# A decoder trunk's attention in another order of steps: the next head's logits first, the splits of k and q alternating between two banks, copies to high parts on GpSimd

## The chip, the cores and the metric

The kernel runs on one core of a Trainium2 chip, in one launch. The metric is the device time of that core in microseconds (us), start to end of the program. A core has TensorE (PE in the rows: matmuls and transposes, written to PSUM), VectorE (DVE), ScalarE (ACT), GpSimd (POOL) and SyncE (SP), which issues the DMAs. Each engine works through its own list of instructions in order and waits on semaphores for the others.

## The reference

Two layers of a decoder trunk on 512 tokens of width 1024, all in float32. Layer 0 mixes tokens with a gated MLP, layer 1 with attention, and each has a SwiGLU feed-forward network. What the change touches is the attention of layer 1:

```python
N_HEADS = 16; HEAD_DIM = 64; Q_BLOCK = 128; S = 512
q, k   = rms_norm(q, q_norm_g), rms_norm(k, k_norm_g)      # per head
gate   = sigmoid(h @ w_qg[:, D:])
logits = q @ k.T * HEAD_DIM**-0.5 + dcum[:, None] - dcum[None, :]
logits = where(key <= query, logits, -inf)
p      = softmax(logits)
o      = p @ v
y      = (o * gate) @ w_o
```

`dcum` is the running sum of log forget gates, one number for each head and token.

## The kernel before, in words

Every float32 matrix product is made of three matmuls in a rounded 32-bit format: each operand is split into a high part (a rounded copy) and a low part (what the rounding left), and high times high, high times low and low times high are summed in PSUM. So nearly every operand costs a copy and a subtraction on an engine besides TensorE.

The attention works on the 16 heads as eight pairs. `v`, `k` (tile `kn`) and `q` (tile `qn`) lie in SBUF with the tokens across the partitions; a pair takes 128 columns. These are the steps, with the names of their tokens in the table `ORDER` and the lines of the kernel before:

- `stack` (token `z0` for k, `z1` for q; L1066 to 1088): four transposes on TensorE (L1071) bring k or q of a pair into one PSUM bank, `ps_z`. Then, for each head of the pair, ScalarE copies the high part (L1085 for k, L1081 for q), VectorE subtracts for the low part (L1086, L1082), and GpSimd copies the high part to a second place (L1087). A small DMA puts the rows of `dcum` below it (L1078). k's bank comes from the two buffers `ps_t`, q's from the two buffers `ps_s`.
- `score` (`s0` to `s3`, one for each block of 128 queries, with 128 to 512 keys; L1090 to 1104): two matmuls into a `ps_s` bank (L1098, L1099); VectorE adds the mask, writes the negated logits `pr` and takes their minimum `mn` (L1102); ScalarE makes the exponentials and their sum (L1103).
- `trans` (`t0` to `t3`, one for each block of 128 keys; L1106 to 1122): transposes of the exponentials (L1113), into `acc` banks for t0 and t1 and `ps_t` banks for t2 and t3; ScalarE copies the high part `pt` (L1120), VectorE subtracts for the low part (L1121).
- `pv` (`v0` to `v3`): probabilities times v (L1133), summed in one `acc` bank for the head.
- `gather` (`g`): the head's result from PSUM to the columns of v that are no longer needed, by a ScalarE copy (L1141) and a VectorE addition (L1142).
- `R`, `T`, `B`: the reciprocals of the sums of both heads of a pair, as three small VectorE instructions (L1147, L1149, L1150), their transposes on TensorE (L1157), copied by ScalarE (L1159), and a matmul that spreads them (L1164), which VectorE multiplies into the gate (L1166).
- `L` and `f`: `gate_mm` loads and splits a pair's gate weights (the high part on VectorE, L118, the low part on GpSimd, L120); their 24 matmuls (L1048) are fillers, handed out one by one wherever an `f` stands. The 24th is followed by the gate's tanh on ScalarE (L1052).
- `V`: `prep_v` splits v of the next pair (L1061 on ScalarE, L1062 on GpSimd). `C`: the gate is multiplied in on GpSimd (L1176). `H`: the result is split for the output projection (L1183 on VectorE, L1184 on GpSimd).

`ORDER` has one line for the even head of a pair and one for the odd head. The loop issues the steps in that order, and `pin` keeps the marked instructions in that order on their engines; unmarked ones (the split of the gate weights) are placed by the scheduler. In the line of head i the score tokens are those of head i+1, and in the line of the even head `z` is the pair after. The loop begins after the projection of q (`moving` over `w_q`), whose head norm is the chain L143 to L154 on VectorE and L981 on GpSimd; the output projection (L1258 to 1260) follows it.

Of the kernel before, what the change touches and what calls it, by code (L numbers as in the profile page):

```python
# [18 lines left out]
P = 128  # L19
D = 1024  # L20
S = 512
# [29 lines left out]


ORDER = (
    "f f B f f f g t1 C f t0 f f V t2 t3 s0 f s1 f f f v0 v1 H s2 s3 v2 z0 v3 f f",
    "f z1 f R L t1 t3 g f f t0 f t2 f T s0 s1 f f f f v0 s2 s3 v1 v2 v3",
)

TRANS_BANK = "aapp"
# [7 lines left out]
def tile_yoco_trunk(ctx: ExitStack, tc: tile.TileContext, x, c, cols, ada_t, kv_ada_t,  # L66
# [799 lines left out]
    with tc.tile_pool(name="att", bufs=1) as tp:  # L866
# [171 lines left out]

        def gate_mm(p_):

            hi, lo = load_split(w_gate[p_], lo_eng=nc.gpsimd, hi_eng=nc.vector)
            box = []

            def step(kt, z):
                if not box:
                    box.append(acc.tile([P, 512], F32, name="acc"))
                cs = slice(kt * P, kt * P + P)
                pin(MM(box[0], (hi, hi, lo)[z][:, cs], h[z == 1][kt], start=kt + z == 0,  # L1048
                       stop=kt == KT - 1 and z == 2))
                if kt == KT - 1 and z == 2:  # L1050
                    ge = tp.tile([P, S], F32, name="ge", bufs=2)
                    pin(ACT(ge, box[0], AF.Tanh, scale=0.5))  # L1052
                    st["ge", p_] = ge
            fill.extend(lambda kt=kt, z=z: step(kt, z) for kt in range(KT) for z in range(3))

        def prep_v(p_):

            cs2 = slice(p_ * P, (p_ + 1) * P)
            vv = tp.tile([P, NT, 4, HD], F32R, name="vv", bufs=2)
            v4 = v[:, :, cs2].rearrange("p n (h d) -> p n h d", d=HD)  # L1060
            pin(ACT(vv[:, :, 0::3, :], v4, AF.Copy))  # L1061
            pin(nc.gpsimd.tensor_tensor(vv[:, :, 1:3, :], v4, f32(vv[:, :, 0::3, :]), sub))  # L1062
            st["vv", p_] = vv
            st["ls", p_] = tp.tile([P, NT, 2], F32, name="lsum", bufs=2)

        def stack(z, p_):  # L1066


            ps = aux.tile([P, NT, P], F32, name="ps_z", tag=("ps_t", "ps_s")[z])
            for n in range(NT):  # L1070
                pin(nc.tensor.transpose(ps[:, n, :], pair((kn, qn)[z], p_)[:, n, :], ident))  # L1071
            for e in range(2):
                i = 2 * p_ + e
                hs = slice(e * HD, (e + 1) * HD)
                src = flat(ps)[hs]
                t1 = tp.tile([P, S], F32R, name=f"st{z}1", bufs=2)
                t2 = tp.tile([HD + 4, S], F32R, name=f"st{z}2", bufs=2)
                nc.sync.dma_start(f32(t2[HD:]), f32(dT[z][4 * i:4 * i + 4]))  # L1078
                if z:
                    hi, dup, lo = (t1[HD:], t2[:HD], t1[:HD]) if e else (t2[:HD], t1[HD:], t1[:HD])  # L1080
                    pin(ACT(hi, src, AF.Copy))  # L1081
                    pin(TT(lo, src, f32(hi), sub))  # L1082
                else:
                    hi, dup, lo = t1[hs], t1[(1 - e) * HD:(2 - e) * HD], t2[:HD]
                    pin(ACT(hi, src, AF.Copy, scale=kqc[hs]))  # L1085
                    pin(STT(lo, src, kqc[hs], f32(hi), mul, sub))  # L1086
                pin(nc.gpsimd.tensor_copy(dup, f32(hi)))  # L1087
                st["kq"[z], i] = t1, t2

        def score(i, n):  # L1090

            p_, e = divmod(i, 2)
            (k1, k2), (q1, q2) = st["k", i], st["q", i]
            ns = slice(n * P, n * P + P)
            w = (n + 1) * P
            wm = max(w, 256)
            ps = aux.tile([P, 512], F32, name="ps_s")
            pin(MM(ps[:, :wm], q1[:, ns], k1[:, :wm], start=True, stop=False))  # L1098
            pin(MM(ps[:, :wm], q2[:, ns], k2[:, :wm], start=False, stop=True))  # L1099
            t = tp.tile([P, w], F32, name=f"pr{n}")  # L1100
            mn = small.tile([P, 1], F32, name="mn", bufs=4)
            pin(nc.vector.tensor_tensor_reduce(t, ps[:, :w], mask[:, S - w:], 1.0, BIG, add, ALU.min, mn))  # L1102
            pin(ACT(t, t, AF.Exp, bias=mn, scale=-1.0, accum_out=st["ls", p_][:, n, e:e + 1]))  # L1103
            st["pr", i, n] = t
# [73 lines left out]
        def close_hl(p_, eng=nc.gpsimd):  # L1178
            o = out_cols(p_)
            if p_ % 4 == 0:  # L1180
                for t in (oh, ol):
                    t.append(outer.tile([P, NT, 512], F32R, name="oh", tag="qk", bufs=4))
            pin(nc.vector.tensor_copy(pair(oh, p_), o))  # L1183
            pin(eng.tensor_tensor(pair(ol, p_), o, f32(pair(oh, p_)), sub))  # L1184

        moving([w_q[0, i] for i in range(4)], KT, 512, hl(h), lambda n, ps: eq(n, ps, 0), n_bg=0)
# [1 line left out]

        def first(i):
            if i == 2:  # L1190
                stack(0, 0)
                stack(1, 0)
            if i == 3:
                for n in range(NT):
                    score(0, n)
        moving([w_q[1, i] for i in range(4)], KT, 512, hl(h), lambda n, ps: eq(n, ps, 1), n_bg=0, extra=first)
        gate_mm(0)
        for i in range(NH):
            p_, e = divmod(i, 2)
            nx, more = i + 1 < NH, p_ + 1 < NH // 2  # L1200
            for tok in ORDER[e].split():
                z = int(tok[1:] or 0)
                tok = tok[0]
                if tok == "f":
                    filler(1)
                elif tok == "z" and more:
                    stack(z, p_ + 1)
                elif tok == "s" and nx:
                    score(i + 1, z)
                elif tok == "t":  # L1210
# [144 lines left out]
```

## Time and profile before

| | |
|---|---|
| time, median of 3 runs | 1394.09 us (1391.73 to 1397.08) |
| profiled execution | 1392.18 us, its span from the first to the last instruction 1390.5 us |
| TensorE busy | 1331.2 us, 96% of the span |
| VectorE, ScalarE, GpSimd busy | 886.3, 577.1, 244.3 us |
| mean granted TensorE clock | 0.988 of full speed |

In the page's forty slices TensorE is below nine tenths in slices 25 to 28 alone, apart from the first; that is the attention. "Busy" of TensorE includes matmuls that run at the lower clock and modelled ends, so the shares of a stretch are read with its granted clock (column PEclk). In rows of a timeline, an entry in square brackets gives how long the engine sat idle before the instruction and what ended that.

### The profile page before, as it was taken

How to read it: one execution, taken by the hardware profiler on the slowest of the kernel's cores; microseconds unless marked ns; L12 is line 12 of the kernel's file. 1: busy time of each engine (PE TensorE's matmuls, PEld its weight loads, DVE VectorE, ACT ScalarE, POOL GpSimd, SP SyncE). 2: the span in 40 equal slices, each digit the busy share in tenths (PEclk: the TensorE clock that was granted, in tenths of full speed). 3: DMA queues.
4: the chain of work that ended last, by engine and by line, in shares of the span. 5: the costliest groups of instructions: out<-in, count | busy, mean ns of one | idle time of the engine just before them, and what ended most of it. 6: DMA issues, size and time to landing. Idle time of an engine off the chain costs nothing.

```text
span 1390.5 us, 17683 instructions
## 1 busy us (share of the span) xinstructions
PE 1331.2 (96%) x6376; PEld 1107.7 (80%) x6376; DVE 886.3 (64%) x1579; ACT 577.1 (42%) x995; POOL 244.3 (18%) x209
## 2 busy tenths in 40 slices
PE   6999999999999999999999998887999999999997
PEld 4788888879888888778898876666789888888886
DVE  7878957666445556563644776666776545446678
ACT  5233432355223232123653456666553222223665
POOL 4700000012111111000110324443112212212000
PEclk9999999999999999999999998999999999999999
DMA  8564436834566666674223330110315777565663
GB/s 326 170 215 155 136 114 197 279 108 126 204 212 198 195 195 217 222 234 128 68 82 99 100 91 17 33 33 17 121 56 184 259 229 244 189 218 165 195 201 129
DMA packets 71336, 221.08 MB, mean 159 GB/s; under 512 B 8657, under 2 KB 8913, under 8 KB 71250
## 3 DMA queue, kind: packets, MB, share of 16 engines
q1 hardware_dynamic: 70674, 218.92, 49.4%
q8 instruction: 50, 0.82, 0.2%
q10 hardware_dynamic: 576, 1.05, 0.2%
q14 instruction: 36, 0.29, 0.1%
HBM read 206.03 MB, written 13.65 MB: 158 GB/s over the span
## 4 chain that ended last, share of the span: by engine, by line
PE 60%; DVE 6%; DMA 5%; ACT 3%; issue 2%; POOL 0%; DVEq 0%; ACTq 0%; SPq 0%
PE acc L535 32%; DMA rawb<-in_ada_t 4%; PE acc L298 4%; PE acc L299 3%; PE acc L300 3%; PE acc L1048 2%; PE acc L1133 1%; PE ps_x L412 1%; PE ps_x L411 1%; PE ps_x L413 1%; PE acc L411 1%; PE acc L412 1%; PE acc L413 1%; PE acc L1259 1%; PE acc L1260 1%
## 5 line engine op out<-in xcount | busy, mean ns | idle before, releaser
L535 PE MATMUL acc<-hT,whi 128*128 128x512 f32 (+1 forms) x1600 | 425.0, 364 | 0.0
L116 ACT ACTIVATE whi<-raw 128x1024 fp32r<-128x1024 f32 (+2 forms) x182 | 189.0, 1041 | 427.2 <-PE acc L535 157.5
L120 DVE TENSOR_TENSOR wlo<-raw,whi 128x1024 fp32r<-128x1024 f32 (+2 forms) x182 | 219.4, 1208 | 160.5 <-ACT whi L116 157.4
L535 PEld LDWEIGHTS acc<-hT,whi 128*128 128x128 f32 x1600 | 276.2, 189 | 47.3
L535 PE MATMUL acc<-hT,wlo 128*128 128x512 f32 (+1 forms) x800 | 263.6, 364 | 0.0
L535 PEld LDWEIGHTS acc<-hT,wlo 128*128 128x128 f32 x800 | 138.8, 189 | 23.8
L182 DVE CUSTOM_DVE_ANT_0 rawb<-rawb,c_bc 128x1024 f32<-128x1024 f32 x59 | 76.0, 1288 | 94.3 <-DMA rawb<-in_ada_t 58.0
L299 PE MATMUL acc<-wlo,hT 128*128 128x512 f32 (+1 forms) x352 | 135.0, 384 | 0.0
L300 PE MATMUL acc<-whi,hT 128*128 128x512 f32 (+1 forms) x352 | 134.7, 383 | 0.0
L298 PE MATMUL acc<-whi,hT 128*128 128x512 f32 (+1 forms) x352 | 134.5, 383 | 0.0
L257 POOL TENSOR_TENSOR hT<-hfull,hT 128x256 fp32r<-128x256 f32 (+1 forms) x43 | 43.6, 1020 | 274.0 <-DVE hT L256 148.0
L299 PEld LDWEIGHTS acc<-wlo,hT 128*128 128x128 f32 x352 | 66.1, 188 | 12.8 <-DVE wlo L120 0.6
L298 PEld LDWEIGHTS acc<-whi,hT 128*128 128x128 f32 x352 | 66.1, 188 | 12.5
L300 PEld LDWEIGHTS acc<-whi,hT 128*128 128x128 f32 x352 | 66.1, 188 | 12.4
L550 POOL TENSOR_TENSOR hid<-sg,hid 128x512 fp32r<-128x512 f32 (+1 forms) x25 | 36.0, 1440 | 193.7 <-ACT hid L549 193.7
L182 DVE CUSTOM_DVE_ANT_0 raw<-raw,c_bc 128x1024 f32<-128x1024 f32 x37 | 46.7, 1263 | 23.8 <-DMA raw<-in_ada_t 23.8
L299 PE MATMUL acc<-wlo,hid 128*128 128x512 f32 x144 | 56.5, 393 | 3.7 <-DVE wlo L120 3.7
L298 PE MATMUL acc<-whi,hid 128*128 128x512 f32 x144 | 56.1, 391 | 1.0 <-ACT junk L325 1.0
L300 PE MATMUL acc<-whi,hid 128*128 128x512 f32 x144 | 56.2, 390 | 0.0
L390 DVE TENSOR_TENSOR hT<-raw,hT 128x512 fp32r<-128x512 f32 x69 | 46.8, 709 | 12.0 <-ACT hT L389 11.6
L120 POOL TENSOR_TENSOR wlo<-raw,whi 128x1024 fp32r<-128x1024 f32 x16 | 44.7, 2793 | 53.6 <-DVE whi L118 47.3
L389 ACT ACTIVATE hT<-raw 128x512 fp32r<-128x512 f32 x69 | 42.0, 625 | 18.0 <-PE ps_x L412 6.5
(334 smaller groups left out, 2415.7 us busy)
## 6 DMA issues: line engine op xcount, KB each, us to landing
raw<-in_w_gu SPq DMA_DIRECT2D x88, 512.0 KB
raw<-in_ada_t SPq DMA_DIRECT2D x53, 512.0 KB
raw<-in_w_down SPq DMA_DIRECT2D x44, 512.0 KB
rawb<-in_ada_t SPq DMA_DIRECT2D x43, 512.0 KB
raw<-in_w_in SPq DMA_DIRECT2D x32, 512.0 KB
raw<-td SPq DMA_DIRECT2D x44, 256.0 KB
raw<-in_w_down SPq DMA_DIRECT2D x33, 256.0 KB
raw<-in_w_out SPq DMA_DIRECT2D x16, 512.0 KB
```

Of the source, the lines that this page charges most:

```text
L116: ACT(hi[:, :width], raw[:, :width], AF.Copy)
L120: lo_eng.tensor_tensor(lo[:, :width], raw[:, :width], f32(hi[:, :width]), sub)
L182: nc.vector.tensor_tensor_reduce(raw, raw, c_bc, 1.0, 0.0, mul, add, dst)
L257: last = lo_eng.tensor_tensor(lo, full, f32(hi), sub)
L298: MM(banks[n], lh, wh, start=kt == 0, stop=False)
L299: MM(banks[n], lh, wl, start=False, stop=False)
L300: MM(banks[n], ll, wh, start=False, stop=kt == kts - 1)
L389: ACT(hi, w, AF.Copy)
L390: TT(lo, w, f32(hi), sub)
L411: MM(bank, ah, wh, start=start, stop=False, skip_group_check=True)
L535: MM(o, (hi, hi, lo)[z][:, ks], h[z == 1][kt][:, cs], start=i == 0, stop=i == 3 * KT - 1)
L550: nc.gpsimd.tensor_tensor(hid[1][m][:, cs], sg, f32(hid[0][m][:, cs]), sub)
```

## The change

- `ORDER` is rewritten: the scores of the next head stand first in the even head's line, and last in the odd head's, where they are interleaved with pv. The token `Z` replaces `z0` and `z1`.
- `stack` makes the transposes of k and q together, and then for each head: high k, high q, low k, low q. So k's `ps_t` bank and q's `ps_s` bank take turns.
- The exponentials `pr` have two buffers instead of one.
- The copies to high parts of v (`prep_v`), of the gate weights (`gate_mm`) and of the result (`close_hl`; but for the last pair) run on GpSimd; before, they ran on ScalarE, VectorE and VectorE.

```diff
 ORDER = (
-    "f f B f f f g t1 C f t0 f f V t2 t3 s0 f s1 f f f v0 v1 H s2 s3 v2 z0 v3 f f",
-    "f z1 f R L t1 t3 g f f t0 f t2 f T s0 s1 f f f f v0 s2 s3 v1 v2 v3",
+    "s0 s1 s2 f f s3 B t3 t2 t1 t0 g f f f f C f f f f Z f V f f f f f v0 v1 L v2 v3",
+    "R f t2 t0 f t1 f f t3 H f g f f T f s0 v0 s1 v1 s2 s3 v2 v3",
 )
 ...
-            hi, lo = load_split(w_gate[p_], lo_eng=nc.gpsimd, hi_eng=nc.vector)
+            hi, lo = load_split(w_gate[p_], lo_eng=nc.gpsimd, hi_eng=nc.gpsimd)
 ...
-            pin(ACT(vv[:, :, 0::3, :], v4, AF.Copy))
+            pin(nc.gpsimd.tensor_copy(vv[:, :, 0::3, :], v4))
 ...
-        def stack(z, p_):
+        def stack(p_):
-            ps = aux.tile([P, NT, P], F32, name="ps_z", tag=("ps_t", "ps_s")[z])
-            for n in range(NT):
-                pin(nc.tensor.transpose(ps[:, n, :], pair((kn, qn)[z], p_)[:, n, :], ident))
+            src = []
+            for t, tag in ((kn, "ps_t"), (qn, "ps_s")):
+                ps = aux.tile([P, NT, P], F32, name="ps_z", tag=tag)
+                for n in range(NT):
+                    pin(nc.tensor.transpose(ps[:, n, :], pair(t, p_)[:, n, :], ident))
+                src.append(flat(ps))
             for e in range(2):
 ...
-                if z:
-                    hi, dup, lo = (t1[HD:], t2[:HD], t1[:HD]) if e else (t2[:HD], t1[HD:], t1[:HD])
-                    pin(ACT(hi, src, AF.Copy))
-                    pin(TT(lo, src, f32(hi), sub))
-                else:
-                    hi, dup, lo = t1[hs], t1[(1 - e) * HD:(2 - e) * HD], t2[:HD]
-                    pin(ACT(hi, src, AF.Copy, scale=kqc[hs]))
-                    pin(STT(lo, src, kqc[hs], f32(hi), mul, sub))
-                pin(nc.gpsimd.tensor_copy(dup, f32(hi)))
+                pin(ACT(k1[hs], k, AF.Copy, scale=kqc[hs]))
+                pin(ACT(qh, q, AF.Copy))
+                pin(STT(k2[:HD], k, kqc[hs], f32(k1[hs]), mul, sub))
+                pin(TT(q1[:HD], q, f32(qh), sub))
+                pin(nc.gpsimd.tensor_copy(k1[ot], f32(k1[hs])))
+                pin(nc.gpsimd.tensor_copy(qd, f32(qh)))
 ...
-            t = tp.tile([P, w], F32, name=f"pr{n}")
+            t = tp.tile([P, w], F32, name=f"pr{n}", bufs=2)
 ...
-            pin(nc.vector.tensor_copy(pair(oh, p_), o))
+            pin(eng.tensor_copy(pair(oh, p_), o))
```

Three places show what moves. In the changed kernel the lines are later by up to two: L1084 and L1085 are the high parts of k and q, L1086 and L1087 the low ones, L1100 and L1101 the scores, L1104 their logits on VectorE, L1123 the low part of the transposed exponentials, L1149 to L1152 the step R, L1159 the step T.

VectorE, around the step R at the end of a pair, before. `st02` and `st11` are the low parts of k and q, `pt0` to `pt3` the four key blocks of the odd head, `r4` the reciprocals that T transposes:

```order
L1086 SCALAR_TENSOR_TENSOR st02_7672<-ps_z_7666,kqc_5912,st01_7671 64x512
L1086 SCALAR_TENSOR_TENSOR st02_7678<-ps_z_7666,kqc_5912,st01_7677 64x512
L1082 TENSOR_TENSOR st11_7693<-ps_z_7688,st12_7694 64x512
L1082 TENSOR_TENSOR st11_7699<-ps_z_7688,st11_7699 64x512
L1147 RECIPROCAL rl_7706<-lsum_7390 128x8
L1121 TENSOR_TENSOR pt1_1_7722<-acc_7717,pt1_0_7721 128x384
L1149 CAST r4_7708<-rl_7706 128x4x2
L1121 TENSOR_TENSOR pt3_1_6305<-ps_t_7725,pt3_0_6304 128x128
L1150 TENSOR_TENSOR r4_7708<-rl_7706,r4_7708 128x4x2
```

The same place now, with `k2` and `q1` for the low parts:

```order
L1144 TENSOR_TENSOR v_5438<-v_5438,acc_7548 64x4x128
L1086 SCALAR_TENSOR_TENSOR k2_7663<-ps_z_7651,kqc_5912,k1_7661 64x512
L1087 TENSOR_TENSOR q1_7662<-ps_z_7656,q2_7664 64x512
L1086 SCALAR_TENSOR_TENSOR k2_7675<-ps_z_7651,kqc_5912,k1_7673 64x512
L1087 TENSOR_TENSOR q1_7674<-ps_z_7656,q1_7674 64x512
L1149 RECIPROCAL rl_7710<-lsum_7466 128x8
L1151 CAST r4_7712<-rl_7710 128x4x2
L1152 TENSOR_TENSOR r4_7712<-rl_7710,r4_7712 128x4x2
L1123 TENSOR_TENSOR pt2_1_7720<-ps_t_7716,pt2_0_7719 128x256
L1123 TENSOR_TENSOR pt0_1_7729<-acc_7723,pt0_0_7728 128x512
```

The two banks `ps_z` now alternate, R stands right behind the splits, and all four low parts of the odd head stand behind R.

TensorE, around T at the end of a pair, before. `st01` to `st12` are the parts of k and q; the scores are those of the next pair's even head:

```order
L1113 MATMUL ps_t_7743<-ident_80,pr3_7660 128x128
L1048 MATMUL acc_7578<-hT_6255,whi_7490 128x512
L1157 MATMUL ps_t_7751<-identr_85,r4_7708 4x128 x4
L1098 MATMUL ps_s_7758<-st01_7671,st11_7693 128x256
L1099 MATMUL ps_s_7758<-st02_7672,st12_7694 128x256
L1098 MATMUL ps_s_7765<-st01_7671,st11_7693 128x256
L1099 MATMUL ps_s_7765<-st02_7672,st12_7694 128x256
L1048 MATMUL acc_7578<-hT_6247,wlo_7492 128x512
```

The end of that pair now, from the last block of scores of the next even head to those of the odd head after it:

```order
L1101 MATMUL ps_s_7790<-k2_7663,q2_7664 128x512
L1135 MATMUL acc_7771<-pt2_0_7719,vv_7463 128x256
L1135 MATMUL acc_7771<-pt2_1_7720,vv_7463 128x256
L1135 MATMUL acc_7771<-pt3_0_6304,vv_7463 128x256
L1135 MATMUL acc_7771<-pt3_1_6305,vv_7463 128x256
L1100 MATMUL ps_s_7801<-k1_7673,q1_7674 128x256
L1101 MATMUL ps_s_7801<-k2_7675,q2_7676 128x256
L1100 MATMUL ps_s_7808<-k1_7673,q1_7674 128x256
L1101 MATMUL ps_s_7808<-k2_7675,q2_7676 128x256
L1100 MATMUL ps_s_7815<-k1_7673,q1_7674 128x384
L1101 MATMUL ps_s_7815<-k2_7675,q2_7676 128x384
L1048 MATMUL acc_7822<-hT_6241,whi_7702 128x512
```

The scores of two heads now follow each other, with no transposes and few fillers between them, through the two `ps_s` banks; the transposes of these exponentials come a head later.

GpSimd, one pair's work before: the gate's low part, the gate multiplied in, the low part of v, and the second places of the high parts.

```order
L120 TENSOR_TENSOR wlo_7044<-raw_7040,whi_7042 128x1024
L1176 TENSOR_TENSOR v_5438<-v_5438,ge_6884 128x4x128
L1062 TENSOR_TENSOR vv_6941<-v_5438,vv_6941 128x4x128
L1087 CAST st01_7000<-st01_7000 64x512
L1087 CAST st01_7006<-st01_7006 64x512
L1087 CAST st11_7022<-st12_7023 64x512
```

One pair's work now:

```order
L1178 TENSOR_TENSOR v_5438<-v_5438,ge_6870 128x4x128
L1088 CAST k1_6992<-k1_6992 64x512
L1089 CAST q1_6993<-q2_6995 64x512
L1088 CAST k1_7004<-k1_7004 64x512
L1089 CAST q2_7007<-q1_7005 64x512
L1061 CAST vv_7017<-v_5438 128x4x2x64
L1062 TENSOR_TENSOR vv_7017<-v_5438,vv_7017 128x4x128
L118 CAST whi_7254<-raw_7252 128x1024
L120 TENSOR_TENSOR wlo_7256<-raw_7252,whi_7254 128x1024
L1185 CAST oh_7299<-v_5438 128x4x128
L1186 TENSOR_TENSOR oh_7300<-v_5438,oh_7299 128x4x128
```

Three casts are new in it (L1061, L118, L1185), and the split of the gate weights stands behind those of k, q and v.

## Rows read from the trace of the kernel before

**Rows 1.** Stretches: first pair, next six pairs, last pair; columns named in its head.
```profile
core 0: us, PE busy (x) PEld busy (x) DVE busy (x) ACT busy (x) POOL busy (x), PEclk, DMA share, GB/s
827.09:844.33 17.24, 12.65 (x65) 10.09 (x64) 13.38 (x35) 10.02 (x25) 10.11 (x10) 0.90 0.10 31
844.33:967.77 123.44, 100.83 (x534) 81.64 (x534) 79.24 (x216) 79.02 (x199) 50.81 (x47) 0.92 0.10 28
967.77:986.41 18.64, 18.55 (x99) 15.23 (x99) 13.20 (x36) 13.56 (x34) 2.58 (x2) 0.91 0.10 29
```

**Rows 2.** Timeline of TensorE: start, us, engine, line, tiles [idle before <-releaser].
```profile
844.33 0.40 PE L1157 MATMUL ps_t<-identr,r 128*4 128x128 f32 x4 [2.54 <-DVE r L1150]
...
922.70 0.41 PE L1113 MATMUL ps_t<-ident,pr 128*128 128x128 f32 x2 [0.85 <-DVE st L1086]
...
925.88 0.40 PE L1157 MATMUL ps_t<-identr,r 128*4 128x128 f32 x4 [2.54 <-DVE r L1150]
...
945.92 0.40 PE L1157 MATMUL ps_t<-identr,r 128*4 128x128 f32 x4 [2.54 <-DVE r L1150]
...
967.77 0.59 PE L1157 MATMUL ps_t<-identr,r 128*4 128x128 f32 x4 [2.54 <-DVE r L1150]
```

**Rows 3.** Stretches of 1 us within one pair, columns as in rows 1.
```profile
924.00:925.00 1.00, 0.00 (x0) 0.00 (x0) 0.95 (x3) 0.98 (x3) 0.61 (x1) 1.00 0.00 0
...
928.00:929.00 1.00, 1.00 (x4) 0.81 (x3) 0.69 (x1) 1.00 (x5) 0.00 (x0) 0.50 0.00 0
...
932.00:933.00 1.00, 1.00 (x4) 0.63 (x4) 0.59 (x1) 0.80 (x3) 0.00 (x0) 1.00 0.21 23
```

**Rows 4.** Chain that ended last, same pair: start, us, what.
```profile
919.64 0.58 ACT st L1085
920.25 0.75 DVE st L1086
921.08 0.69 ACT st L1085
...
922.58 0.69 DVE st L1082
923.36 0.60 ACT st L1081
...
925.88 0.40 PE ps_t L1157 x4
```

**Rows 5.** Groups by line, six pairs (844.33:967.77): busy, mean ns | idle before, releaser.
```profile
L1103 ACT ACTIVATE pr<-pr,mn 128x128 f32<-128x128 f32 (+3 forms) x48 | 26.8, 558 | 24.4 <-DVE mn L1102 24.4
...
L1102 DVE CUSTOM_DVE_ANT_0 pr<-ps_s,mask 128x128 f32<-128x128 f32 (+3 forms) x48 | 21.7, 484 | 8.2 <-PE ps_s L1099 8.2
...
L1087 POOL CAST st<-st 64x512 fp32r<-64x512 f32 x24 | 14.6, 609 | 20.6 <-ACT st L1085 14.8 <-ACT st L1081 5.5
L120 POOL TENSOR_TENSOR wlo<-raw,whi 128x1024 fp32r<-128x1024 f32 x6 | 14.3, 2386 | 28.0 <-DVE whi L118 22.6 <-PE ps_s L1099 5.3
...
L1142 DVE TENSOR_TENSOR v<-v,acc 64x512 f32<-64x512 f32 x13 | 8.9, 681 | 0.2
...
L1062 POOL TENSOR_TENSOR vv<-v,vv 128x512 fp32r<-128x512 f32 x6 | 7.8, 1295 | 1.8 <-ACT vv L1061 1.8
...
L118 DVE CAST whi<-raw 128x1024 fp32r<-128x1024 f32 x6 | 4.2, 694 | 2.6 <-PE acc L1048 1.9 <-issue 0.6
...
L1061 ACT ACTIVATE vv<-v 128x512 fp32r<-128x512 f32 x6 | 3.7, 622 | 0.0
...
L1183 DVE CAST oh<-v 128x512 fp32r<-128x512 f32 x5 | 2.1, 424 | 3.9 <-PE ps_z L1071 3.9
...
L1149 DVE CAST r<-rl 128x8 fp32r<-128x8 f32 x6 | 1.0, 162 | 0.0
```

**Rows 6.** Timeline of GpSimd in the first pair, columns as in rows 2.
```profile
828.51 2.39 POOL L120 TENSOR_TENSOR wlo<-raw,whi 128x1024 fp32r<-128x1024 f32 x1 [4.95 <-DVE whi L118]
830.85 1.28 POOL L1062 TENSOR_TENSOR vv<-v,vv 128x512 fp32r<-128x512 f32 x1
```

**Rows 7.** Timeline of VectorE in the same stretch.
```profile
829.13 1.80 DVE L143 TENSOR_SCALAR rs<-s 128x32 f32<-128x32 f32 x1
830.97 1.20 DVE L146 TENSOR_SCALAR r<-rs 128x32 int32<-128x32 int32 x1
...
832.56 0.17 DVE L147 TENSOR_TENSOR rs<-r 128x32 f32<-128x32 f32 x1
```

More of the change, by code (lines that the diff above doesn't have):

```diff
@@ L1072, in stack @@
             for e in range(2):
                 i = 2 * p_ + e
[L1074 to L1078, printed above, removed]
-                if z:
-                    hi, dup, lo = (t1[HD:], t2[:HD], t1[:HD]) if e else (t2[:HD], t1[HD:], t1[:HD])
-                    pin(ACT(hi, src, AF.Copy))
-                    pin(TT(lo, src, f32(hi), sub))
-                else:
-                    hi, dup, lo = t1[hs], t1[(1 - e) * HD:(2 - e) * HD], t2[:HD]
-                    pin(ACT(hi, src, AF.Copy, scale=kqc[hs]))
-                    pin(STT(lo, src, kqc[hs], f32(hi), mul, sub))
@@ L1087, in stack @@
-                pin(nc.gpsimd.tensor_copy(dup, f32(hi)))
-                st["kq"[z], i] = t1, t2
+                hs, ot = slice(e * HD, (e + 1) * HD), slice((1 - e) * HD, (2 - e) * HD)
+                (k1, q1), (k2, q2) = ([tp.tile([w, S], F32R, name=f"{s_}{j}", bufs=2) for s_ in "kq"]
+                                      for j, w in ((1, P), (2, HD + 4)))
+                for z, t in enumerate((k2, q2)):
+                    nc.sync.dma_start(f32(t[HD:]), f32(dT[z][4 * i:4 * i + 4]))
+                qh, qd = (q1[HD:], q2[:HD]) if e else (q2[:HD], q1[HD:])
@@ L1090, in score @@
+                k, q = (x[hs] for x in src)
+                pin(ACT(k1[hs], k, AF.Copy, scale=kqc[hs]))
[4 more added lines that the diff above has]
+                pin(nc.gpsimd.tensor_copy(qd, f32(qh)))
+                st["k", i], st["q", i] = (k1, k2), (q1, q2)
         def score(i, n):
@@ L1190, in first @@
             if i == 2:
-                stack(0, 0)
-                stack(1, 0)
+                stack(0)
             if i == 3:
@@ L1205, in tile_yoco_trunk @@
                     filler(1)
-                elif tok == "z" and more:
-                    stack(z, p_ + 1)
+                elif tok == "Z" and more:
+                    stack(p_ + 1)
                 elif tok == "s" and nx:
```

## The prediction

> **What bounds the kernel now.** I read the page's slices first: TensorE is nine tenths busy or more nearly everywhere except in the attention, so only there has a new order of steps something to win. Then I read the attention by stretches [rows 1]. The marker is the step T, the transposes of the reciprocals, once in each pair. From the first T to the seventh there are six periods in 123.44 us, 20.57 us each; a plain one is 945.92 - 925.88 = 20.04 [rows 1, 2]. In none of the four engines is a period full: TensorE 100.83 / 6 = 16.8 us busy, VectorE 13.2, ScalarE 13.2, GpSimd 8.5 [rows 1]. So what bounds a pair is waiting, and TensorE's own share must be cleaned of the clock: the granted clock over the stretch is 0.92, and since the clock has two levels, 1.2 and 2.4 GHz, 16% of the time, 3.3 us a pair, was at the lower one. The work done in those 3.3 us would take 1.65 us at the higher. So the period holds 20.57 - 3.77 idle - 1.65 = 15.15 us of TensorE work at full clock.
>
> Where the idle 3.77 us sits is read from TensorE's timeline: 0.85 us before the transposes t2, and 2.54 us before T, the latter the same in all four rows shown [rows 2]. Both end on VectorE. The chain shows why: ScalarE's high part, VectorE's low part, ScalarE's next high part, each starting 0.03 to 0.08 us after the other has ended [rows 4]. Both heads' parts lie in one PSUM bank, and each engine waits until the other has left it; four rounds of that last from 919.64 to about 924, and the odd head's exponentials and the reciprocals stand behind them in the queues of both engines. TensorE is still for the whole of 924 to 925, then its clock is at 0.50 (1.2 GHz) at 928, and back at 1.00 by 932 [rows 3]. So one jam costs a pair about 5.4 us: the idle time and the clock behind it.
>
> **The change part by part.** *The splits.* The eight instructions stay, 4 x 0.6 to 0.7 us on ScalarE and 4 x 0.7 on VectorE [rows 4], but k's and q's banks alternate, so ScalarE makes high q while VectorE subtracts k. Four rounds of 1.4 us become a pipeline of some 3.6. The splits also start right behind the transposes, with 16 of the pair's 24 fillers and four steps of pv around them, and TensorE needs their result only at the next pair's scores. The two waits of TensorE in rows 2 lose their cause.
>
> *The logits.* Scores of two heads now follow each other through two ps_s banks: VectorE needs 8 x 0.484 = 3.9 us for them, ScalarE 8 x 0.558 = 4.5 us for the exponentials [rows 5]. TensorE has about as much to do meanwhile (16 score matmuls, one head's pv, two fillers). What waits behind a score for its bank is the list of TensorE, and what is late then is the transposes, which need these exponentials only a head later (hence two pr buffers). I count short waits, under 1 us each.
>
> *The casts.* VectorE loses 0.69 and, in five of six periods, 0.42; ScalarE loses 0.62 [rows 5]: 12.2 and 12.55 us remain. GpSimd gains a cast of 1024 columns and two of 512 on 128 partitions, which the trace does not show. The nearest row is 0.61 us for 64 x 512; two-operand work on 128 partitions takes 1.30 for 512 columns and 2.39 for 1024 [rows 5]. So the three together cost between 2.4 and 5.0 us; I take 2.4, as the row is of the same kind of copy. GpSimd has then 10.9 us a period, 13.5 at the worst, under the 15.15 either way, and nothing of it is wanted at once, except the second places of k and q, which go before the other casts.
>
> *The step H.* In two of the six periods its cast waited for transposes of k, 3.9 us in all [rows 5], since the result takes k's buffer. H now stands after the transposes; such a period (967.77 - 945.92 = 21.85 us [rows 2]) becomes a plain one.
>
> *The step R.* This is what the move costs. R's cast and subtraction are 0.16 us when GpSimd is quiet [rows 5]. In the first pair, VectorE's small L143 and L146 took 1.80 and 1.20 us, ending as GpSimd's instructions of 2.39 and 1.28 us ended, and L147, with GpSimd idle, 0.17 [rows 6, 7]. In the new order R falls where GpSimd copies k, q and v without a pause. I take 1.0 us: one cast of 0.61 and the rest of another. Behind R on VectorE stand the odd head's four low parts, and T and pv wait for them. The bounds are 0 and twice 2.39 = 4.8 us. The Trainium skill, SBUF — State Buffer, section "Who interferes with whom", gives the mechanism: GpSimd and VectorE share a port pair that one instruction holds to its end, and a VectorE cast, or an operation with two SBUF inputs against a reading GpSimd, waits for it. The trace agrees (1.80 and 1.20 us); by that rule alone R could wait for two whole instructions, which is the slower rival.
>
> *The new period.* The longest loop is ScalarE's: 12.55 us of work; 0.9 waiting for the last logits; 0.3 for VectorE to leave a bank (a low part of 0.75 beside a high part of 0.60); 1.0 from R; and some twenty handoffs between engines at 0.03 to 0.08 [rows 4], 1.0. That makes 15.75, above TensorE's 15.15; since both miss each other now and then I take 16.0. TensorE's idle time is then under 1 us at each place, so I count the full clock.
>
> *The sum.* Six periods: 6 x (20.57 - 16.0) = 27.4 us. The first pair, 17.24 us: the chain L143 to L154 now stands ahead of the second head's logits on VectorE, and the gate's splits on GpSimd get in its way as in rows 6 and 7; the third score, ready by 828 and held until the chain that starts at 829.13 is through, will wait some 5 us, while the splits get shorter. I take a gain of 1.5, between a loss of 2 and a gain of 4. The last pair with its tail, 18.64 us: it has no splits; its granted clock of 0.91 means 3.4 us at the lower level, 1.7 us to win [rows 1]; I take 2, between 0 and 4. Together 30.9. The profiled execution took 1392.18 us (1390.5 of span and 1.7 around it), the median of the runs is 1.9 above it: 1394.1 - 30.9 = 1363.
>
> **The rivals.** *A: half of it comes back.* The two ps_s banks become the new jam: TensorE waits at nearly each of the eight scores for VectorE, and the idle pieces bring the lower clock back. For it: 8.2 us that VectorE already waits for scores in six periods [rows 5], so the hand-over of a bank is not free. Against it: pv and fillers stand between. Price: 1.65 us for the clock and 0.55 for waits, 18.2 us a pair, 6 x 2.4 = 14.2, with 1 for the ends: 1379.
>
> *B: slower.* GpSimd holds R. Each pair's cast and subtraction wait for a long GpSimd instruction each, 2.39 us twice, and the lower clock stays: 16.0 - 1.0 + 4.8 + 1.65 = 21.45 us a pair, 5.3 more than before in six periods, and 2 lost in the first pair: 1401. For it: rows 6 and 7, and the gate's split now wholly on GpSimd. Against it: that split comes last in its order, behind k, q and v. It decides from a wait of 3.9 us at R, with the lower clock.
>
> *C: the change does not do what it says.* If ScalarE and VectorE are still kept in turn, by the copies on GpSimd or a wait that the order does not show, the period stays within 1 us of 20: 1388 to 1394.
>
> **How the numbers follow.** My forecast, 1363, has 0.72; its own range goes from 1351 (period 14.5, which needs TensorE's modelled ends to overstate its work, and 6 from the ends) to 1374 (period 17.2, ends 0). A has 0.15, B 0.06, C 0.05, and 0.02 lies below 1351. Holding eight of ten, the range takes in A's middle: 1351 to 1380. Two runs of this kernel can differ by about 0.5%, 7 us, without a cause: faster than 1387 has 0.72 + 0.15 + 0.01 + 0.02 = 0.90, the same 0.04 (most of C), slower 0.06 (B).
>
> **What would show it.** In the profile after, T follows T by 15 to 17 us; TensorE's idle time before T and t2 is under 1 us; the granted clock of the six periods is 0.97 or more; VectorE's subtractions of k and q start while ScalarE copies the other bank. R's cast or subtraction shows 0.3 to 1.3 us instead of 0.16. GpSimd is at 10 to 12 us a pair. I am wrong if the clock still falls once in each pair, if scores wait for banks more than 2 us a pair, or if R's two instructions take more than 3 us; and the casts are mispriced if the one of 1024 columns takes over 2 us.

## The result and the profile after

The changed kernel takes 1363.57 us (median of 4 runs, 1362.82 to 1365.59), beside 1395.14 us for the kernel before on the same chip: a ratio of 0.9778, with a 95% interval of 0.9758 to 0.9797. The forecast was 1363. The profiled execution took 1365.59 us, its span 1363.9. The sum behind the forecast is less exact than its end: one term is too small, two are too large.

The stretches of the profile after, cut at the same places as [rows 1]: from the loop's start to the first T, to the seventh T, to the first matmul of the output projection. The columns are those of [rows 1].

```profile
core 0: us, PE busy (x) PEld busy (x) DVE busy (x) ACT busy (x) POOL busy (x), PEclk, DMA share, GB/s
830.34:849.86 19.52, 14.16 (x69) 12.02 (x67) 12.91 (x34) 9.11 (x23) 11.69 (x12) 0.83 0.09 28
849.86:942.11 92.25, 91.79 (x536) 75.33 (x535) 77.02 (x204) 75.26 (x193) 60.98 (x62) 1.00 0.13 37
942.11:960.47 18.36, 16.93 (x97) 13.54 (x95) 15.28 (x36) 13.56 (x33) 7.03 (x8) 1.00 0.09 30
```

Six periods went from 123.44 to 92.25 us, 20.57 to 15.38 each. TensorE is busy for 91.79 of the 92.25 at a granted clock of 1.00: within 0.1 us a pair it now does nothing but work. The first pair lost 2.28 us (17.24 to 19.52, clock 0.83), and the last gained 0.28. These three make 29.19 us; the spans differ by 26.6 us, as 2.6 us were lost in code that the change leaves as it was (L930, which stands ahead of the attention, already starts 3.4 us later, at 724.7 instead of 721.3).

TensorE around one T, after. Against [rows 2] the idle time in brackets is gone, before t2 (the transposes at 908.88) and before T (L1159), and the fillers L1048 stand between the transposes:

```profile
908.66 0.39 PE L1048 MATMUL acc<-hT,whi 128*128 128x512 f32 x1
908.88 0.38 PE L1115 MATMUL ps_t<-ident,pr 128*128 128x128 f32 x2
...
910.90 0.63 PE L1048 MATMUL acc<-hT,whi 128*128 128x512 f32 x2
911.37 0.40 PE L1159 MATMUL ps_t<-identr,r 128*4 128x128 f32 x4
```

VectorE in that pair, the splits of k and q and then R. The four subtractions take 906.51 to 909.71, 3.2 us. Before, the first and the last of the four stood here, 4.4 us from start to end (920.25 to 924.68):

```profile
920.25 0.74 DVE L1086 SCALAR_TENSOR_TENSOR st<-ps_z,kqc,st 64x512 fp32r<-64x512 f32 x1 [1.52 <-ACT st L1085]
...
923.99 0.69 DVE L1082 TENSOR_TENSOR st<-ps_z,st 64x512 fp32r<-64x512 f32 x1 [0.72 <-ACT st L1081]
```

And now:

```profile
906.51 0.74 DVE L1086 SCALAR_TENSOR_TENSOR k<-ps_z,kqc,k 64x512 fp32r<-64x512 f32 x1 [0.31 <-ACT k L1084]
907.18 0.67 DVE L1087 TENSOR_TENSOR q<-ps_z,q 64x512 fp32r<-64x512 f32 x1
908.35 0.76 DVE L1086 SCALAR_TENSOR_TENSOR k<-ps_z,kqc,k 64x512 fp32r<-64x512 f32 x1 [0.49 <-ACT k L1084]
909.02 0.69 DVE L1087 TENSOR_TENSOR q<-ps_z,q 64x512 fp32r<-64x512 f32 x1
...
909.96 0.17 DVE L1151 CAST r<-rl 128x8 fp32r<-128x8 f32 x1
910.17 0.57 DVE L1152 TENSOR_TENSOR r<-rl,r 128x8 fp32r<-128x8 f32 x1
```

ScalarE at the same time: the second copy, of q (906.38), runs to 906.96, while VectorE reads k from 906.51. The banks do alternate.

```profile
905.80 0.69 ACT L1084 ACTIVATE k<-ps_z,kqc 64x512 fp32r<-64x512 f32 x1 [0.44 <-PE ps_z L1073]
906.38 0.58 ACT L1085 ACTIVATE q<-ps_z 64x512 fp32r<-64x512 f32 x1
907.63 0.69 ACT L1084 ACTIVATE k<-ps_z,kqc 64x512 fp32r<-64x512 f32 x1 [0.67 <-POOL v L1178]
```

Groups of the six periods, to be read against [rows 5]: count, busy time, mean ns, then the idle time before.

```profile
L1105 ACT ACTIVATE pr<-pr,mn 128x128 f32<-128x128 f32 (+3 forms) x48 | 26.9, 560 | 5.6 <-DVE mn L1104 4.6
L1104 DVE CUSTOM_DVE_ANT_0 pr<-ps_s,mask 128x128 f32<-128x128 f32 (+3 forms) x48 | 23.2, 489 | 8.2 <-PE ps_s L1101 6.6 <-ACT pr L1105 0.3
...
L1100 PEld LDWEIGHTS ps_s<-k,q 128*128 128x128 f32 x48 | 9.0, 187 | 4.4 <-DVE mn L1104 2.6
...
L118 POOL CAST whi<-raw 128x1024 fp32r<-128x1024 f32 x6 | 6.2, 1039 | 0.3 <-PE acc L1048 0.3
...
L1061 POOL CAST vv<-v 128x512 fp32r<-128x512 f32 x5 | 3.2, 633 | 0.3
L1185 POOL CAST oh<-v 128x512 fp32r<-128x512 f32 x5 | 3.0, 608 | 10.9 <-PE ps_z L1073 10.9
...
L1151 DVE CAST r<-rl 128x8 fp32r<-128x8 f32 x6 | 2.5, 422 | 0.2
L1152 DVE TENSOR_TENSOR r<-rl,r 128x8 fp32r<-128x8 f32 x6 | 1.9, 312 | 0.2
```

ScalarE's wait for the logits' minima fell from 24.4 to 4.6 us: the logits no longer come late. The three casts take 1.04, 0.63 and 0.61 us. H's wait is longer than before (10.9 us in two pairs, not 3.9), but it stands on GpSimd now, and the two periods with it (15.36 and 15.30 us) are like the others.

### The profile page after: what moved, and what is told of

It is laid out like the page before. It is cut to its first block, busy times and chain, and to the rows that moved or that the text cites. A ratio compares the mean times of both kernels' runs of the same rounds, so it can differ in the third digit from the quotient of the medians.

```text
span 1363.9 us, 17591 instructions
## 1 busy us (share of the span) xinstructions
PE 1325.7 (97%) x6376; PEld 1104.2 (81%) x6376; DVE 886.3 (65%) x1564; ACT 572.0 (42%) x987; POOL 263.1 (19%) x232
## 5 line engine op out<-in xcount | busy, mean ns | idle before, releaser
L120 DVE TENSOR_TENSOR wlo<-raw,whi 128x1024 fp32r<-128x1024 f32 (+2 forms) x182 | 220.1, 1212 | 173.6 <-ACT whi L116 171.8
L120 POOL TENSOR_TENSOR wlo<-raw,whi 128x1024 fp32r<-128x1024 f32 x16 | 44.7, 2794 | 21.1 <-DVE whi L118 20.5
```

What stands on the lines that cost most here:

```text
L120: lo_eng.tensor_tensor(lo[:, :width], raw[:, :width], f32(hi[:, :width]), sub)
```

## The experiments

All twelve runs, with the three stretches of each kernel's profiled execution cut as above (for the six periods, the mean in brackets). Ratios are to the kernel before, with 95% intervals.

| kernel | median us | ratio | first pair | six periods | last pair |
|---|---|---|---|---|---|
| before | 1394.1 | | 17.24 | 123.44 (20.57) | 18.64 |
| changed | 1363.6 | 0.978 (0.976–0.980) | 19.52 | 92.25 (15.38) | 18.36 |
| 1 copies back | 1363.7 | 0.977 (0.975–0.979) | 12.86 | 96.26 (16.04) | 18.35 |
| 2 copies alone | 1392.8 | 0.998 (0.997–1.000) | 17.37 | 122.84 (20.47) | 18.75 |
| 3 alternation alone | 1375.5 | 0.986 (0.984–0.988) | 16.33 | 106.71 (17.79) | 18.75 |
| 4 no alternation | 1369.7 | 0.982 (0.980–0.984) | 19.14 | 99.12 (16.52) | 17.72 |
| 5 less TensorE work | 1355.2 | 0.972 (0.970–0.975) | 17.53 | 88.99 (14.83) | 15.43 |
| 6 fillers ahead | 1385.8 | 0.994 (0.993–0.996) | 17.25 | 118.10 (19.68) | 17.68 |
| 7 first gate copy back | 1356.2 | 0.973 (0.971–0.976) | 12.19 | 91.98 (15.33) | 18.20 |
| 8 as 7, w_o on GpSimd | 1355.2 | 0.972 (0.970–0.975) | 12.18 | 92.25 (15.38) | 16.82 |
| 9 as 8, own first order | 1356.8 | 0.973 (0.971–0.975) | 13.68 | 92.31 (15.39) | 16.83 |
| 10 gate split behind Z | 1365.3 | 0.978 (0.976–0.980) | 20.75 | 92.19 (15.37) | 18.20 |
| 11 as 10, R later | 1373.5 | 0.986 (0.984–0.988) | 21.53 | 101.08 (16.85) | 18.62 |
| 12 changed, again | 1365.0 | 0.977 (0.975–0.979) | 19.38 | 92.27 (15.38) | 18.31 |

**1. The changed kernel, copies to high parts put back.**

```diff
-            hi, lo = load_split(w_gate[p_], lo_eng=nc.gpsimd, hi_eng=nc.gpsimd)
+            hi, lo = load_split(w_gate[p_], lo_eng=nc.gpsimd, hi_eng=nc.vector)
-            pin(nc.gpsimd.tensor_copy(vv[:, :, 0::3, :], v4))
+            pin(ACT(vv[:, :, 0::3, :], v4, AF.Copy))
-            pin(eng.tensor_copy(pair(oh, p_), o))
+            pin(nc.vector.tensor_copy(pair(oh, p_), o))
```

> The changed kernel, with the three copies to high parts back on ScalarE (v) and VectorE (gate weights, result); order and alternation stay. Theory (order and alternation remove the jam, TensorE is then the bound, and the casts matter little): VectorE goes from 12.84 to some 13.9 us a pair, ScalarE from 12.54 to 13.2, GpSimd from 10.2 to 7.9, all still under TensorE's 15.15, so the period stays at 15.4 to 15.9 and the kernel within 4 us of the changed kernel's 1364. Rival (VectorE and ScalarE are the bound, so moving their copies to GpSimd is what gained): a period of 16.5 or more, and 1371 or more.

The time is that of the changed kernel, 1363.7, as the theory had it. But the period, 16.04, lies between the theory's range and the rival's, and the time is a sum of two effects with opposite signs, 4.0 and 6.7 us (the 2.7 between them is within what single runs differ by). In the six periods the copies on GpSimd gain 4.0 us (96.26 to 92.25). The rows of VectorE show how: the unpinned gate copy (L118) falls among the next head's logits, and the fourth score waits for the bank. Four such waits, 0.74 to 0.80 us each, make 3.0 of the 3.9 us that TensorE idles in these six periods; in the changed kernel it idles 0.5.

```profile
893.26 1.20 DVE L118 CAST whi<-raw 128x1024 fp32r<-128x1024 f32 x1
894.38 0.41 DVE L1104 CUSTOM_DVE_ANT_0 pr<-ps_s,mask 128x256 f32<-128x256 f32 x1
```

TensorE in the same place:

```profile
894.86 0.50 PE L1100 MATMUL ps_s<-k,q 128*128 128x512 f32 x1 [0.74 <-DVE mn L1104]
```

In the first pair the same copies cost 6.7 us (19.52 against 12.86). Experiment 7 takes that up.

**2. The kernel before, with only the copies on GpSimd** (the same three lines, the other way).

> The kernel before, with only the three copies to high parts moved to GpSimd; old order, old sequence of splits. Theory: the jam is in the splits of k and q and stays; the wait of the step H leaves VectorE's list, 3.9 us in two of six periods, of which TensorE may feel 1 to 3. So 1388 to 1394, and the two waits of TensorE before T and t2 and the half clock are still there. Rival (relief of VectorE and ScalarE is what gained): 1380 or less.

1392.8, a period of 20.47. The jam is there, T waits 2.74 to 2.80 us in each pair. As a change of its own, the copies are worth next to nothing.

**3. The kernel before, with only the alternation.** The transposes of k and q stay where they were, and the eight split instructions follow the second:

```diff
-                    pin(ACT(hi, src, AF.Copy, scale=kqc[hs]))
-                    pin(STT(lo, src, kqc[hs], f32(hi), mul, sub))
+            if not z:
+                return
+                ...
+                pin(ACT(kh, sk, AF.Copy, scale=kqc[hs]))
+                pin(ACT(qh, sq, AF.Copy))
+                pin(STT(kl, sk, kqc[hs], f32(kh), mul, sub))
+                pin(TT(ql, sq, f32(qh), sub))
```

> The kernel before, with only the sequence of the splits changed: those of k wait for the transposes of q, and then the two banks take turns; TensorE's order, its steps and the casts are as before. Theory (the jam is the two engines waiting for one bank, but it is also in the wrong place): the four rounds of 5.4 us shrink by some 1.5 us, the wait of 2.54 us before T to about 1, with part of the half clock: a period of 18 to 19.5, 1380 to 1387. Rival 1 (the place alone matters): 1390 to 1395. Rival 2 (alternation alone matters): a period under 16.5, 1368 or less.

1375.5, better than the theory had it (1380 to 1387) and short of rival 2 (1368 or less). The stop before T (here L1163) went from 2.54 to 1.02 us, as expected, and that before t2 stays at 0.86:

```profile
861.93 0.40 PE L1163 MATMUL ps_t<-identr,r 128*4 128x128 f32 x4 [1.02 <-DVE r L1156]
```

What was underrated is the clock behind the stop, which stays at 1.00 in five of the six periods. Three of the six are shown, the last with H's wait in it:

```profile
844.96:861.93 16.97, 15.09 (x89) 12.42 (x89) 12.65 (x36) 13.06 (x34) 7.32 (x7) 1.00 0.11 35
...
880.43:898.96 18.53, 16.64 (x90) 13.65 (x90) 13.09 (x37) 13.02 (x34) 8.62 (x8) 0.91 0.11 31
...
932.90:951.67 18.77, 15.72 (x90) 12.32 (x90) 12.98 (x37) 12.87 (x34) 8.59 (x8) 1.00 0.10 31
```

**4. The changed kernel, with the old sequence of splits** (k, k, q, q; all else as changed):

```diff
+            for hs, ot, k, q, k1, k2, q1, qh, qd in parts:
+                pin(ACT(k1[hs], k, AF.Copy, scale=kqc[hs]))
+                pin(STT(k2[:HD], k, kqc[hs], f32(k1[hs]), mul, sub))
+                ...
+            for hs, ot, k, q, k1, k2, q1, qh, qd in parts:
+                pin(ACT(qh, q, AF.Copy))
+                pin(TT(q1[:HD], q, f32(qh), sub))
```

> The changed kernel, with only the sequence of the splits undone: both parts of k first, then both of q, so that ScalarE and VectorE wait for each other's bank again; order of steps and casts as in the changed kernel. Theory (most of the gain is the place of the splits, with 16 fillers and pv around them): the splits take about 2 us longer, R, the low parts and T come later, TensorE waits under 1 us a pair: 15.4 to 16.5 us a pair, 1364 to 1371. Rival (alternation is what gained): the wait before T is back at over 2 us with the half clock, 18 us a pair or more, 1379 or more.

1369.7, 16.52 a pair, at the upper end of the theory's range. The four subtractions take 908.14 to 912.57, 4.4 us, as in the kernel before, and T waits for the low parts behind them:

```profile
897.47 0.40 PE L1162 MATMUL ps_t<-identr,r 128*4 128x128 f32 x4 [0.77 <-DVE pt L1126]
```

Read together, 3 and 4 show that the gain has two causes that overlap. Alternation alone takes 2.78 us off the period; the new order with the copies, but without alternation, 4.05; all together 5.19, not 6.8. Both remove the same jam, one by shortening the splits, the other by giving TensorE work until they are done. Alternation is worth 2.78 in the old order and 1.14 in the new. The second buffer of `pr` is in each run of the new order, so its own share is not shown.

**5. The changed kernel with less work for TensorE.**

```diff
+                cut = 512 if z == 0 else 256
-                pin(MM(box[0], (hi, hi, lo)[z][:, cs], h[z == 1][kt], start=kt + z == 0,
+                pin(MM(box[0][:, :cut], (hi, hi, lo)[z][:, cs], h[z == 1][kt][:, :cut], start=kt + z == 0,
```

> The changed kernel with less work on TensorE: of the 24 gate matmuls of a pair, the 16 that bring the low parts in go over 256 columns instead of 512 (that half of the gate's correction is left out); order, waits and the work of the other engines stay. That is 16 x 0.11 = 1.8 us less TensorE work a pair. Theory (TensorE is the bound at 15.15 to 15.4 us): the period falls to some 13.8 to 14.5, limited by VectorE's 12.8 and its waits; six pairs 6 to 9 us shorter, 1351 to 1358 with the two ends. Rival (the loop of ScalarE or VectorE is the bound, as the forecast had it at 15.75): the period stays over 15, TensorE just idles, 1360 or more.

The period is 14.83, just above the range that the theory gave and just under the rival's. The period did fall, so TensorE was the bound; but only by 0.54 of the 1.36 us by which TensorE's busy time fell (1.8 was expected), since the next bound stands right behind. The rows of the six periods and of a T show it: TensorE now idles 5.4 us in six pairs, most of it before T, for VectorE's low parts.

```profile
844.36:933.35 88.99, 83.63 (x534) 69.87 (x535) 76.54 (x205) 74.34 (x194) 61.44 (x63) 1.00 0.13 39
```

```profile
874.08 0.40 PE L1160 MATMUL ps_t<-identr,r 128*4 128x128 f32 x4 [0.92 <-DVE pt L1124]
```

So the loop through ScalarE and VectorE, which the prediction took for the bound at 15.75, is at most some 14.8 long.

**6. The kernel before, with four fillers moved ahead of T.**

```diff
-    "f z1 f R L t1 t3 g f f t0 f t2 f T s0 s1 f f f f v0 s2 s3 v1 v2 v3",
+    "f z1 f R L t1 t3 g f f t0 f t2 f f f f f T s0 s1 v0 s2 s3 v1 v2 v3",
```

> The kernel before, with only four fillers of the odd head moved from behind its second score step (s1) to ahead of T, so that TensorE has 0.9 us of work where it stood still for 2.54 us; splits, banks and casts as before. Theory (the jam costs by its stop and by the lower clock after it): the wait before T falls to 1.6 us. The run with alternation alone showed no lower clock in five of six periods after a stop of 1.0 us, so it may go in part here too: a gain of 0.9 to 2.5 us a pair, period 18 to 19.7, 1380 to 1389. Rival (the fillers only change places, and TensorE waits where they stood, at pv or the third score): the period stays over 20.2, 1391 or more.

The stop is 1.61 to 1.63 us in all periods, and 1385.8 the time. It also prices the clock: its four periods without H's wait hold the same stops before t2 (0.85 us) and T, and differ in the clock.

```profile
846.24:864.40 18.16, 15.61 (x89) 12.29 (x89) 12.71 (x36) 12.94 (x34) 7.41 (x7) 1.00 0.11 32
...
885.60:905.21 19.61, 17.09 (x89) 13.66 (x89) 13.24 (x37) 13.03 (x34) 8.69 (x8) 0.91 0.11 30
905.21:923.38 18.17, 15.62 (x89) 12.28 (x89) 13.05 (x37) 12.94 (x34) 8.69 (x8) 1.00 0.10 32
923.38:942.87 19.49, 16.99 (x89) 13.59 (x90) 13.24 (x37) 13.03 (x34) 8.69 (x8) 0.91 0.11 29
```

18.17 against 19.55: the fall of the clock costs a pair 1.4 us, where the prediction had worked out 1.65 from its mean. In the kernel before, all six periods have 0.91 or 0.92.

**7. The changed kernel, first pair's gate copy back on VectorE.**

```diff
-            hi, lo = load_split(w_gate[p_], lo_eng=nc.gpsimd, hi_eng=nc.gpsimd)
+            hi, lo = load_split(w_gate[p_], lo_eng=nc.gpsimd, hi_eng=nc.gpsimd if p_ else nc.vector)
```

> The changed kernel, with one copy put back: the high part of the first pair's gate weights is made on VectorE, that of the other seven pairs on GpSimd. Theory (in the first pair the scheduler put the whole chain L143 to L154 ahead of the second head's logits, and it did so for the changed kernel with that copy on GpSimd, not for the one with the copies back): the logits stand ahead of the chain again, the third score waits under 1 us, and the first pair takes 13 us instead of 19.5; the six periods stay at 15.4: 1355 to 1359. Rival (the first pair's loss is from the order of the steps itself, scores before transposes): no change, 1362 to 1365.

1356.2, and the first pair takes 12.19 us. In the changed kernel the whole chain L143 to L154 stands ahead of the second head's logits on VectorE; its first instruction takes 1.69 us beside GpSimd's low part of the gate weights (L120, 831.69 to 834.03):

```profile
832.38 1.69 DVE L143 TENSOR_SCALAR rs<-s 128x32 f32<-128x32 f32 x1
...
835.88 0.19 DVE L154 SCALAR_TENSOR_TENSOR r<-rs,r 128x32 f32<-128x32 f32 x1
835.99 0.28 DVE L1104 CUSTOM_DVE_ANT_0 pr<-ps_s,mask 128x128 f32<-128x128 f32 x1
```

TensorE there: the third score waits 5.36 us, and its 0.69 us for 384 columns (0.44 behind the short wait of experiment 7) is the lower clock, granted at 0.50 from 836 to 842.

```profile
836.34 0.69 PE L1100 MATMUL ps_s<-k,q 128*128 128x384 f32 x1 [5.36 <-DVE mn L1104]
```

In experiment 7, the logits of the first three scores stand ahead of the chain and the third score waits 0.34 us:

```profile
829.51 0.44 PE L1100 MATMUL ps_s<-k,q 128*128 128x384 f32 x1 [0.34 <-DVE mn L1104]
```

```profile
830.45 0.55 DVE L1104 CUSTOM_DVE_ANT_0 pr<-ps_s,mask 128x384 f32<-128x384 f32 x1
...
830.93 1.38 DVE L143 TENSOR_SCALAR rs<-s 128x32 f32<-128x32 f32 x1
```

One copy's engine decides how the scheduler mixes two unrelated lists on VectorE. Why it does, these runs do not show.

**8. As 7, with the first piece of the output projection's weights split on GpSimd** (`lo_eng=nc.gpsimd, hi_eng=nc.gpsimd` for the first `load_split` of `w_o`).

> As the kernel before this (first pair's gate copy on VectorE), and the first piece of the output projection's weights is split on GpSimd, not on ScalarE and VectorE, so that its 1.74 us on VectorE do not stand among the last pair's logits. Theory (that subtraction makes the fourth score of the last pair wait 1.34 us): the last pair takes 17.0 to 17.4 us instead of 18.36, 1 us or a little more less than the kernel without it: 1354 to 1358. Rival (GpSimd's longer split, 1.04 + 2.40 us, holds VectorE's casts or the projection's start instead): no gain, 1356 to 1361.

The last pair takes 16.82 us instead of 18.20, a little under the theory's 17.0 to 17.4. In the changed kernel the piece's low part stands between the logits, and the fourth score waits 1.34 us:

```profile
943.64 1.74 DVE L120 TENSOR_TENSOR wlo<-raw,whi 128x1024 fp32r<-128x1024 f32 x1
945.31 0.41 DVE L1104 CUSTOM_DVE_ANT_0 pr<-ps_s,mask 128x256 f32<-128x256 f32 x1
```

TensorE in the same place:

```profile
945.78 0.50 PE L1100 MATMUL ps_s<-k,q 128*128 128x512 f32 x1 [1.34 <-DVE mn L1104]
```

The median, 1355.2, is 1.0 under that of 7, less than the runs of either differ among themselves. Both beat the kernel before and the changed one.

**9. As 8, with an order of its own for the first head** (`s0 s1 t3 t2 t1 t0`, twelve `f`, then `s2 f s3` and the rest).

> The kernel with the first pair's gate copy on VectorE and the first piece of the output projection's weights on GpSimd, and an order of its own for the first head: the second head's first two scores, then all transposes of the first head and twelve fillers, then the other two scores, so that TensorE has work while VectorE has the chain L143 to L154. Theory (the first pair is already at 12.2 us with TensorE busy for 11.5 of them): at most 0.7 us less than without this order, 1353 to 1357, which is the same within what these runs can tell. Rival (the chain still delays the first pair): 1350 or less. A loss by the transposes' low parts standing between the logits: 1358 or more.

1356.8: no gain; the first pair is 1.5 us longer than in 8, and TensorE waits 1.14 us before its T.

**10. The changed kernel, with L right behind Z** (`Z L f V ... v0 v1 v2 v3`).

> The changed kernel, with only the step L (the load and split of the next pair's gate weights) moved from near the end of the even head's line to right behind Z, so that on GpSimd the cast of 1024 columns and the subtraction of 2.4 us stand right behind the copies of k and q, where VectorE has R. Theory (GpSimd's instruction holds VectorE's cast and two-input subtraction until it ends, and R cost little in the changed kernel only because short copies stand there): R's cast takes up to 1.0 us and its subtraction up to 2.4, some 2 to 3 us for the two instead of 0.7; T and the odd head's low parts come that much later, VectorE's loop of 14.8 us becomes 16.5 to 17.5 and TensorE waits 1 to 2 us before T: 1370 to 1383. Rival (nothing is held, R was slow for another reason): R stays under 1 us, the period 15.4, 1362 to 1366.

1365.3 with periods of 15.37: no difference, but the run decides nothing. The gate's cast began at 910.52, 1.3 us after R had ended (909.19), so the two never met. Experiment 11 moves R instead.

**11. As 10, with R moved behind t1.**

```diff
-    "R f t2 t0 f t1 f f t3 H f g f f T f s0 v0 s1 v1 s2 s3 v2 v3",
+    "f t2 t0 f t1 R f f t3 H f g f f T f s0 v0 s1 v1 s2 s3 v2 v3",
```

> As the run with the step L right behind Z, and the step R moved three key blocks later in the odd head's line (behind t1). In that run R was over 1.5 us before GpSimd began the gate's cast, and met nothing long; now R's cast should start within some 0.3 us of that cast's start. Theory (GpSimd's instruction holds VectorE's cast or two-input subtraction until it ends): in pairs where they meet, R's cast takes up to 1.0 us or its subtraction up to 2.4, T follows their end, and TensorE stops 1 to 3 us before T: a period of 16 to 18.5, 1368 to 1384. Rival (no hold): R's two instructions stay at 0.17 us each, T waits under 0.6 us for their later place, 15.4 to 15.8 a pair: 1363 to 1368.

1373.5, five periods of 17.0, as the theory had it. R's cast takes 0.99 us and ends as GpSimd's ends (862.87 + 0.99 = 863.86; 862.80 + 1.04 = 863.84). In the last pair of that stretch GpSimd has no such cast there, and R's takes 0.17. VectorE:

```profile
862.87 0.99 DVE L1151 CAST r<-rl 128x8 fp32r<-128x8 f32 x1
863.90 0.17 DVE L1152 TENSOR_TENSOR r<-rl,r 128x8 fp32r<-128x8 f32 x1
...
947.81 0.17 DVE L1151 CAST r<-rl 128x8 fp32r<-128x8 f32 x1
```

GpSimd, beside the first of these:

```profile
862.80 1.04 POOL L118 CAST whi<-raw 128x1024 fp32r<-128x1024 f32 x1 [1.62 <-issue]
```

TensorE at the two T:

```profile
864.21 0.40 PE L1159 MATMUL ps_t<-identr,r 128*4 128x128 f32 x4 [1.54 <-DVE r L1152]
...
948.34 0.40 PE L1159 MATMUL ps_t<-identr,r 128*4 128x128 f32 x4 [0.72 <-DVE r L1152]
```

The stop is 0.72 us from R's later place and 0.82 more where the cast is held, which is what the cast lost (0.99 - 0.17). GpSimd's subtraction of 2.39 us began only at 865.04, so R did not meet it, and a hold of that length stays untried.

**12. The changed kernel again**, beside 10.

> The changed kernel once more, beside the run above on the same chip. Every theory: 1362 to 1366, and six periods of 15.4 us.

1365.0 and 15.38 a period: the stretches repeat within 0.15 us.

## Why the prediction was right, point by point

*The bound and the jam.* Right. (One of the page's forty slices before is below nine tenths besides those named, the last: the end of the program, not the attention.) Taking the splits' two engines out of each other's way and out of TensorE's way removes the stops in [rows 2] and the clock's fall in [rows 3]; experiments 3, 4 and 6 show each by itself, experiment 2 that the copies are not it. The splits' four rounds took 5.0 us before (919.64 to 924.68), not four times 1.4, and take 3.9 now (905.80 to 909.71), forecast 3.6.

*The new period.* 15.38, forecast 16.0: the term of six periods was 27.4 and measured 31.2. The step that failed is the one that set ScalarE's loop, 15.75, above TensorE's work, 15.15, and so took the loop for the bound. With TensorE relieved, the loop closes within 14.83 (experiment 5). Of the 0.9 us too much, 0.6 is R: 1.0 was counted, and the cast and subtraction take 0.42 + 0.31 where 0.32 was usual, 0.4 more. Where the rest lies stays open; the terms for the bank and the handoffs were not measured by themselves. The 0.25 us added because the two miss each other was not needed: TensorE idles 0.08 us a pair. ScalarE's wait for logits was counted right (0.9; 4.6 / 6 = 0.77), and so was its work (12.55; 75.26 / 6 = 12.54). TensorE's work at full clock, 15.15, measured 15.30.

*R.* The mechanism is shown, the size was off. What R meets in the new order are copies of 0.61 us, or the end of one: in the six periods its cast takes 0.17 us once and 0.39 to 0.58 in the others, its subtraction 0.17 four times and about 0.6 twice. In the last pair of the changed kernel the cast meets GpSimd's multiplication by the gate (L1178) and ends 0.03 us after it, at 955.15:

```profile
954.02 1.13 DVE L1151 CAST r<-rl 128x8 fp32r<-128x8 f32 x1
```

```profile
953.83 1.29 POOL L1178 TENSOR_TENSOR v<-v,ge 128x512 f32<-128x512 f32 x1 [9.53 <-DVE v L1144]
```

In experiment 11, where it meets one of 1.04 us squarely, it loses 0.82. The Trainium skill, SBUF — State Buffer, section "Who interferes with whom", says of a VectorE instruction in a two-port mode, which a cast can enter, and one of GpSimd that the later "fully blocks" while the first holds the shared ports. The ends of the two casts in experiment 11, 0.02 us apart, agree.

*The casts.* 1.04 + 0.63 + 0.61 = 2.28 us a pair, forecast 2.4: the near row was the right end of 2.4 to 5.0. What I did not count is where an unpinned instruction of that kind stands on VectorE: the three copies off ScalarE and VectorE are worth 0.67 us a pair (experiment 1), and the waits behind the gate copy make 0.5 of it.

*H.* Its periods are like the others now, as forecast. The wait did not vanish, it moved to GpSimd, where it does not lengthen the period.

*The first pair.* A gain of 1.5 was forecast, with -2 as the worst; it lost 2.28. The wait of the third score was foreseen at "some 5 us" (5.36), but priced without the clock: over 19.52 us at 0.83, 6.6 us ran at the lower level, where the kernel before has 3.4 of 17.24. That is 1.6 us more. Nor did I see that the chain's place follows from one copy (experiment 7: 12.19 us).

*The last pair.* A gain of 2 was forecast, 0.28 came. The clock did rise, 0.91 to 1.00; the new waits, 18.36 - 16.93 = 1.43 us, took its place, nearly all of it the weights of the next step among the logits (experiment 8).

*The rivals.* A: two `ps_s` banks are no jam, the score's weight load waited 2.6 us for VectorE in six pairs. B: experiment 11 makes 0.82 of its 4.8 us at R real, and shows how it would come about. C fell with the first T. The ends lost 5.5 us against the forecast, the periods gained 3.8 over it, and the unchanged code and the spread of the runs make up the rest. So the jam and what removes it were right, but that the time came within 1 us of the forecast is luck: two errors of opposite sign.

## What to carry to other kernels

A jam between two engines over one PSUM bank can be removed by shortening it or by putting work beside it; the two gains overlap, so each must be tried alone before they are added. When TensorE stops, price the clock after the stop with the stop. Where a scheduler places some instructions, look at what a moved copy does to the lists of the other engines, at the first and last turn of a loop above all.

## What was not expected of the hardware

The clock answers to stops in no simple way. With stops of 2.54 to 2.80 us before T it fell in each of the twelve periods of the kernel before and of experiment 2 (granted clock 0.87 to 0.92); with 1.54 us before T (experiment 11) the six periods show 1.00. After 0.85 us before t2 and 1.62 before T (experiment 6) it fell three times and stayed once, with the same stops to 0.02 us. In experiment 3, after at most 0.86 and 1.04 us, it stayed five times, and it fell both times that H had lengthened the stop before t2 to 1.43 us (the period from 880.43, and the last pair, at 0.91 each). What decides between falling and staying, with the same stops, stays open.
